# Order of the attention tiles in a hybrid decoder trunk: NSA, DSA, NSA, DSA in place of NSA, NSA, DSA, DSA

## The chip, the cores and the metric

The kernel runs on one core of a Trainium2 chip. The metric is the time of one execution on the device in microseconds, the median of three runs.

## The reference

Two layers work on 256 tokens of width 1024 in float32. A layer normalizes x (RMSNorm), projects it to 5472 columns, runs two causal token mixers side by side, adds their gated sum to x, and then adds a SwiGLU feed-forward of width 2816. The mixers, cut to what matters here:

```python
def _nsa_mixer(...):            # 8 heads, 2 key/value groups
    # compressed keys: 15 blocks of 32 tokens, stride 16; then the selected blocks and the window
    p_c = _masked_softmax(s_c, cmp_end <= t);  o_c = p_c @ vc
    p_s = _masked_softmax(q @ k_slc * ATTN_SCALE, causal);  o_s = p_s @ v_slc
    p_w = _masked_softmax(q @ k_win * ATTN_SCALE, causal);  o_w = p_w @ v_win
    return g0 * o_c + g1 * o_s + g2 * o_w

def _dsa_mixer(...):            # 8 heads
    # the indexer scores all keys, the best 64 of a query stay
    score = sum_h relu(iq_h @ ik) * iw_h;  sel = top_k(score, 64)
    return softmax(q @ k[sel] * ATTN_SCALE) @ v[sel]

def _hybrid_mixer(...):
    y_nsa = _nsa_mixer(...) @ w_branch_nsa
    y_dsa = _dsa_mixer(...) @ w_branch_dsa
    merged = sigmoid(gate_nsa) * y_nsa + sigmoid(gate_dsa) * y_dsa
    return merged @ w_out
```

With 256 tokens all four selection blocks are taken, and the window covers everything, so "selected" and "window" are plain causal attention over two sets of keys and values.

## The kernel before

The 256 tokens are two tiles of 128. Every large matrix product is made of three float32 matmuls: weights and activations are split into a high and a low half, and `mul3` (lines 194 to 196) issues high times high, low times high and high times low. ScalarE makes the high half of a weight tile (line 185), VectorE the low half (line 186). Raw weight tiles have five buffers, the halves four.

A layer's first part runs in this order of the source: the indexer's projection and the selection of keys, the projections of the NSA mixer, its compressed keys and values, the projections `dq`, `dk` and `dv` of the DSA mixer, then the attention itself, the projections of the two gates (line 727 evacuates them), the branch products (`branch`, `br` 0 for NSA and 1 for DSA; lines 749 and 751 evacuate them), and the output product.

`nsa(i)` handles one tile of tokens of the NSA mixer: the compressed scores (line 615), then groups of scores (line 368) into two PSUM banks `sc`, each followed by `softmax`; at the end the value matmuls (line 664 and, for the compressed part, line 667) into the only bank `yv`, and `y_out`, which splits the result into `ya` (lines 606, 607). The first tile sees 128 keys and makes four softmaxes, the second 256 keys and makes eight. `dsa(i)` does the same for the DSA mixer: scores (line 686 for the first tile, line 368 for the second), two softmaxes for the first tile and four for the second, value matmuls (line 703), `y_out`.

`softmax` is, on VectorE, a pass that adds the bias, scales and finds the maximum (line 330), on ScalarE the exponential with its sum (line 333), on VectorE the reciprocal and the scaling (lines 340, 342), then four transposes on TensorE (line 313) and their copy into a tile `pt` (line 314). There are eight tiles `pt`; a mixer's tile of tokens keeps its own until its value matmuls are done. The value matmuls of `nsa` begin with the `pt` that is made last.

The second tile of `dsa` multiplies split operands: `stack` and `twice` build `dks` and `dqs` (lines 351 to 362) in the memory of the tiles `qs` and `ks`, which `nsa` reads, so they can be written only when the last scores of `nsa(1)` are done. The first tile of `dsa` reads `dqT` and `dkT` unsplit and needs neither.

The order on each engine is made by a planner when the program is built: it takes what its own estimate says is ready, earlier lines of the source first. Blocks marked `manual_schedule` keep their order on TensorE among themselves; other work may come between.

Of the kernel before, what the change touches and what calls it, by code (L numbers as in the profile page):

```python
# [18 lines left out]
NT = SEQ // P  # L19
# [58 lines left out]
def hybrid_trunk(ctx: ExitStack, tc: tile.TileContext, a: dict, out: bass.AP):  # L78
# [17 lines left out]
    def yv_bank():  # L96
        return bank("yv", 1)
# [4 lines left out]
    def sc_bank():  # L102
        return bank("sc", 2)
# [216 lines left out]
    def softmax(segs, bias, gate):  # L320


        n, nb = len(segs), len(segs) and 4 // len(segs)
        pr = work.tile([P, n, nb * P], F32, tag="pr", name="pr", bufs=8)
        mx = small.tile([P, n], F32, tag="mx", name="mx")
        sm = small.tile([P, n], F32, tag="sm", name="sm")
        c = small.tile([P, n], F32, tag="c", name="c")
        b3 = bias.rearrange("p (b t) -> p b t", t=P)
        for h, v in enumerate(segs):
            nc.vector.tensor_tensor_reduce(pr[:, h].rearrange("p (b t) -> p b t", t=P), v, b3,  # L330
                                           -0.125, 3.4e38, ALU.add, ALU.min, accum_out=mx[:, h:h + 1])
        for h in range(n):
            nc.scalar.activation(pr[:, h], pr[:, h], AF.Exp, bias=mx[:, h:h + 1], scale=-1.0,  # L333
                                 accum_out=sm[:, h:h + 1])
        if gate is None:
            nc.vector.tensor_scalar_max(sm, sm, 1e-30)
        else:
            nc.vector.scalar_tensor_tensor(sm.rearrange("p (a b) -> p a b", b=2), sm.rearrange("p (a b) -> p a b", b=2),
                                           1e-30, gate, ALU.max, ALU.mult)
        nc.vector.reciprocal(c, sm)  # L340
        for h in range(n):
            nc.vector.tensor_scalar_mul(pr[:, h], pr[:, h], c[:, h:h + 1])  # L342
        pt = work.tile([P, 4, P], F32, tag="pt", name="pt", bufs=PTB)
        transpose_into(pt, [pr[:, h, b * P:(b + 1) * P] for h in range(n) for b in range(nb)])
        return pt
# [9 lines left out]
    def twice(dh, dl, src):  # L355

        for e in range(2):
            nc.scalar.activation(dh[e][HALF[e]], src[HALF[e]], AF.Copy)
            nc.any.tensor_copy(dh[e][HALF[1 - e]], src[HALF[e]])
        for e in range(2):  # L360
            for h in (e, 1 - e):
                nc.vector.tensor_sub(dl[e][HALF[h]], src[HALF[e]], dh[e][HALF[e]].bitcast(F32))

    def score(o, q, k):

        pairs = [(q, t) for t in k] if isinstance(k, (list, tuple)) else [(t, k) for t in q]
        for n, (u, v) in enumerate(pairs):
            nc.tensor.matmul(o, u, v, start=n == 0, stop=n == 1)  # L368
# [14 lines left out]
    for l in range(DEPTH):  # L383
# [220 lines left out]
        def y_out(bank, k0, tok):  # L604
            y3 = bank.rearrange("p (k t) -> p k t", t=P)
            nc.any.tensor_copy(ya[0][:, k0:k0 + 4, tok], y3)
            nc.vector.tensor_sub(ya[1][:, k0:k0 + 4, tok], y3, ya[0][:, k0:k0 + 4, tok].bitcast(F32))
# [60 lines left out]
                                 pct[:, 0], start=False, stop=r == 3)  # L668
            y_out(yn, 0, tok)

        def dsa(i):
            tok = slice(i * P, (i + 1) * P)
            nk = P * (i + 1)
            per = 512 // nk
            yd = yv_bank()

            done = []
            for p0 in range(0, 4, per):
                pts = []
                sbs = [sc_bank() for _ in range(2)]  # L680
                if i == 0:

                    with tc.manual_schedule(engines={nc.tensor.engine}):
                        for p in range(4):
                            for e in (1, 0):
                                nc.tensor.matmul(sbs[e][:, p * P:(p + 1) * P], dqT[HALF[e], p, 0:P],
                                                 dkT[HALF[e], p, 0:P], start=True, stop=True)
                else:
                    for p in range(p0, p0 + per):
                        for e in range(2):  # L690
                            score(sbs[e][:, (p - p0) * nk:(p - p0 + 1) * nk], [dqs[:, z, p] for z in (e, 2 + e)],
                                  dks[:, e, p])
                for sb in sbs:
                    segs = sb.rearrange("p (h b t) -> p h b t", h=per, t=P)
                    pts.append(softmax([segs[:, h] for h in range(per)], dbias[i], None))
                done.append((p0, pts))
            with tc.manual_schedule(engines={nc.tensor.engine}):
                for p in range(3, -1, -1):
                    p0, pts = done[p // per]
                    for b in range(i + 1):  # L700
                        for e in (1, 0):
                            v0 = (2 * p + e) * 64
                            nc.tensor.matmul(yd[e * 64:(e + 1) * 64, p * P:(p + 1) * P], dv[:, b, v0:v0 + 64],  # L703
                                             pts[e][:, (p - p0) * (i + 1) + b], start=p == 3 and b == 0,
                                             stop=p == 0 and b == i)
            y_out(yd, 4, tok)

        for i in range(NT):
            nsa(i)

        dks = one.tile([P, 2, 4, SEQ], F32R, tag="qs", name="dks")
        dqs = one.tile([P, 4, NT, 2 * P], F32R, tag="ks", name="dqs").rearrange("p z b (c t) -> p z (b c) t", t=P)
        stack([dks[:, e] for e in range(2)], dkT)
        twice([dqs[:, e] for e in range(2)], [dqs[:, 2 + e] for e in range(2)], dqT[:, :, P:])
        dsa(0)
        dsa(1)


        rhalf = []
# [186 lines left out]
```

## Time and profile before

| | |
|---|---|
| median of 3 runs | 800.53 us (799.58 to 800.77) |
| the profiled execution | 799.6 us, its span 797.8 us |
| TensorE, VectorE, ScalarE busy | 99%, 69%, 58% |
| mean granted clock of TensorE | 0.997 |

The span runs from the first to the last instruction of the profiled execution. PE is TensorE, PEld its weight loads, DVE VectorE, ACT ScalarE. Busy times of matmuls overlap, and their ends are modelled. In a timeline a row gives the start, how long the row lasts, the engine, the line, the operation, what it writes from what it reads, and how many instructions it joins. A row of windows gives the stretch, its length, then the busy time of PE, PEld, DVE, ACT and POOL with the number of instructions, the granted clock, the share of the DMA engines and GB/s; engines that a filtered answer doesn't have are left out.

### The profile page before, as it was taken

To read this page: it belongs to the slowest core of one execution; us is meant where nothing else is said; L and a number is where in the kernel's file an instruction comes from. 1 tells how busy PE (TensorE), PEld (TensorE's weight loads), DVE (VectorE), ACT (ScalarE), POOL (GpSimd) and SP (SyncE) were. 2 spreads that over 40 slices of the span, in tenths; PEclk is the share of its full clock that TensorE was granted. 3 is DMA by queue.
4 is the path that set the end of the run, shared out by engine and by line. 5 is a ranking of instruction groups with operands and counts; after the bars stand their busy time and mean duration, and the time that the engine had idled before them with its cause. 6 is when DMAs were issued, how large, how long until landed. Compare 5 with 4: busy or idle time off the path is not lost.

```text
span 797.8 us, 11520 instructions
## 1 busy us (share of the span) xinstructions
PE 788.3 (99%) x4122; PEld 655.3 (82%) x4122; DVE 547.0 (69%) x1187; ACT 460.5 (58%) x792; POOL 9.1 (1%) x18
## 2 busy tenths in 40 slices
PE   9999999999999999999999999999999999999996
PEld 6888888888888888888888888888888888888884
DVE  6789888967756455654567997989676555655544
ACT  6767577865645444543566756777557444545442
POOL 0100000000000000000000000000000000000000
PEclk9999999999999999999999999999999999999998
DMA  9964565324565556565468456442363666555651
GB/s 297 355 228 144 163 181 132 106 85 145 186 205 179 180 183 187 182 206 190 141 207 282 155 159 185 132 132 81 106 228 118 194 200 209 184 167 180 209 160 53
DMA packets 76282, 139.97 MB, mean 175 GB/s; under 512 B 7057, under 2 KB 22417, under 8 KB 76225
## 3 DMA queue, kind: packets, MB, share of 16 engines
q1 hardware_dynamic: 75120, 136.95, 55.0%
q10 hardware_dynamic: 864, 1.57, 0.5%
q0 software_dynamic: 240, 0.72, 0.3%
q8 instruction: 32, 0.52, 0.3%
q14 instruction: 26, 0.20, 0.1%
HBM read 138.17 MB, written 1.05 MB: 175 GB/s over the span
## 4 chain that ended last, share of the span: by engine, by line
PE 98%; DMA 0%; ACT 0%; DVE 0%; POOLq 0%; issue 0%; SPq 0%; ACTq 0%
PE mm L196 26%; PE mm L194 26%; PE mm L195 26%; PE tr L313 2%; PE sc L368 2%; PE yv L196 2%; PE yv L194 2%; PE yv L195 2%; PE yv L664 1%; PE tr L833 1%; PE yv L703 1%; PE tr L267 1%; PE yv L667 1%; PE sc L194 1%; PE sc L195 0%; PE sc L556 0%
## 5 line engine op out<-in xcount | busy, mean ns | idle before, releaser
L186 DVE TENSOR_TENSOR lo<-raw,hi 128x1024 fp32r<-128x1024 f32 (+2 forms) x252 | 299.5, 1195 | 140.8 <-ACT hi L185 135.6
L185 ACT ACTIVATE hi<-raw 128x1024 fp32r<-128x1024 f32 (+2 forms) x252 | 259.8, 1037 | 166.7 <-PE mm L196 112.6
L195 PE MATMUL mm<-lo,ah 128*128 128x512 f32 (+1 forms) x786 | 306.3, 390 | 0.0
L194 PE MATMUL mm<-hi,ah 128*128 128x512 f32 (+1 forms) x786 | 305.4, 394 | 0.0
L196 PE MATMUL mm<-hi,al 128*128 128x512 f32 (+1 forms) x786 | 305.3, 391 | 0.0
L196 PEld LDWEIGHTS mm<-hi,al 128*128 128x128 f32 x786 | 147.5, 188 | 29.6 <-issue 0.5
L195 PEld LDWEIGHTS mm<-lo,ah 128*128 128x128 f32 x786 | 147.8, 188 | 28.3 <-issue 0.3
L194 PEld LDWEIGHTS mm<-hi,ah 128*128 128x128 f32 x786 | 147.7, 188 | 28.3 <-issue 0.2
L333 ACT ACTIVATE pr<-pr,mx 128x128 f32<-128x128 f32 (+1 forms) x96 | 42.5, 445 | 11.4 <-DVE mx L330 11.1
L196 PE MATMUL mm<-hi,hl 128*128 128x512 f32 x126 | 49.1, 389 | 0.0
L195 PE MATMUL mm<-lo,hh 128*128 128x512 f32 x126 | 49.0, 389 | 0.0
L194 PE MATMUL mm<-hi,hh 128*128 128x512 f32 x126 | 48.8, 393 | 0.0
L838 DVE TENSOR_TENSOR hl<-tr,hh 128x512 fp32r<-128x512 f32 (+1 forms) x24 | 15.5, 647 | 38.3 <-ACT hh L837 38.3
L837 ACT ACTIVATE hh<-tr 128x512 fp32r<-128x512 f32 (+1 forms) x24 | 13.5, 562 | 47.2 <-PE tr L833 47.2
L196 PEld LDWEIGHTS mm<-hi,hl 128*128 128x128 f32 x126 | 23.6, 188 | 5.0
L195 PEld LDWEIGHTS mm<-lo,hh 128*128 128x128 f32 x126 | 23.7, 188 | 4.7
L194 PEld LDWEIGHTS mm<-hi,hh 128*128 128x128 f32 x126 | 23.7, 188 | 4.7
L342 DVE TENSOR_SCALAR pr<-pr,c 128x128 f32<-128x128 f32 (+1 forms) x96 | 25.1, 315 | 0.6
L824 ACT ACTIVATE sg<-mm,rstd 128x512 f32<-128x512 f32 (+1 forms) x24 | 15.7, 654 | 10.5 <-PE mm L196 8.7
L330 DVE CUSTOM_DVE_ANT_0 pr<-sc,cst 128x128 f32<-128x128 f32 (+1 forms) x64 | 19.5, 352 | 2.6 <-PE sc L368 2.4
L314 ACT COPY pt<-tr 128x512 f32<-128x512 f32 x32 | 17.7, 584 | 4.9 <-PE tr L313 4.7
L313 PE MATMUL tr<-cst,pr 128*128 128x128 f32 x144 | 20.0, 272 | 0.0
(237 smaller groups left out, 757.8 us busy)
## 6 DMA issues: line engine op xcount, KB each, us to landing
raw<-w_in SPq DMA_DIRECT2D x76, 512.0 KB, 4.0
raw<-w_ffn_down SPq DMA_DIRECT2D x44, 512.0 KB, 4.1
raw<-w_ffn_gate SPq DMA_DIRECT2D x40, 512.0 KB, 4.5
raw<-w_ffn_up SPq DMA_DIRECT2D x40, 512.0 KB, 4.3
raw<-w_out SPq DMA_DIRECT2D x16, 512.0 KB, 4.5
raw<-w_branch_nsa SPq DMA_DIRECT2D x16, 256.0 KB, 4.0
raw<-w_branch_dsa SPq DMA_DIRECT2D x8, 512.0 KB, 3.6
raw<-w_in SPq DMA_DIRECT2D x8, 280.0 KB, 3.9
```

Source lines behind the costliest of these rows:

```text
L185: nc.scalar.activation(hi[:, cs], raw[:, cs], AF.Copy)
L186: nc.vector.tensor_sub(lo[:, cs], raw[:, cs], hi[:, cs].bitcast(F32))
L194: nc.tensor.matmul(dst, xh, wh, start=first, stop=False)
L195: nc.tensor.matmul(dst, xh, wl, start=False, stop=False)
L196: nc.tensor.matmul(dst, xl, wh, start=False, stop=last)
L313: nc.tensor.transpose(tp[:, k * P:(k + 1) * P], piece, ident)
L314: nc.any.tensor_copy(dst, tp[:, 0:len(parts) * P].rearrange("p (k t) -> p k t", t=P))
L330: nc.vector.tensor_tensor_reduce(pr[:, h].rearrange("p (b t) -> p b t", t=P), v, b3, -0.125, 3.4e38, ALU.add, ALU.min, accum_out=mx[:, h:h ...
L333: nc.scalar.activation(pr[:, h], pr[:, h], AF.Exp, bias=mx[:, h:h + 1], scale=-1.0, accum_out=sm[:, h:h + 1])
L342: nc.vector.tensor_scalar_mul(pr[:, h], pr[:, h], c[:, h:h + 1])
L368: nc.tensor.matmul(o, u, v, start=n == 0, stop=n == 1)
L824: nc.scalar.activation(s[:, 0:n], dg[i][:, 0:n], AF.Silu, scale=rstd[i])
```

## The change

The four attention tiles are called in the order NSA first token tile, DSA first, NSA second, DSA second. Before, both tiles of NSA came first. The stacked copies `dks` and `dqs` are still made after the second tile of NSA, and `dsa` gets them as arguments, since its first call now stands ahead of them. Both layers are changed alike.

```diff
-        def dsa(i):
+        def dsa(i, dqs=None, dks=None):
...
-        for i in range(NT):
-            nsa(i)
+        nsa(0)
+        dsa(0)
+        nsa(1)
 
         dks = one.tile([P, 2, 4, SEQ], F32R, tag="qs", name="dks")
         dqs = one.tile([P, 4, NT, 2 * P], F32R, tag="ks", name="dqs").rearrange("p z b (c t) -> p z (b c) t", t=P)
         stack([dks[:, e] for e in range(2)], dkT)
         twice([dqs[:, e] for e in range(2)], [dqs[:, 2 + e] for e in range(2)], dqT[:, :, P:])
-        dsa(0)
-        dsa(1)
+        dsa(1, dqs, dks)
```

## Rows read from the trace of the kernel before

**Rows 1.** The page: busy engines and the clock in 40 slices.
```profile
PE 788.3 (99%) x4122; PEld 655.3 (82%) x4122; DVE 547.0 (69%) x1187; ACT 460.5 (58%) x792; POOL 9.1 (1%) x18
...
PEclk9999999999999999999999999999999999999998
```

**Rows 2.** Timeline of TensorE: the opening, and the projections near 98 us.
```profile
1.19 3.64 PE L110 MATMUL tr<-zeros 128*128 128x512 bf16 x10 [1.19 <-DVE warm L135]
...
98.17 0.39 PE L195 MATMUL mm<-lo,ah 128*128 128x512 f32 x1
98.40 0.39 PE L196 MATMUL mm<-hi,al 128*128 128x512 f32 x1
```

**Rows 3.** All waits of TensorE: us in total, times, longest.
```profile
PE tr L110 <- DVE warm L135: 1.2, 1, 1.2
PE sc L194 <- ACT hi L185: 0.7, 1, 0.7
```

**Rows 4.** Windows: the opening, and two stretches of layer 1's attention.
```profile
0.00:3.90 3.90, 2.71 (x7) 1.04 (x8) 0.43 (x7) 1.27 (x1) 0.20 (x4) 1.00 0.49 162
...
93.00:143.00 50.00, 50.00 (x284) 41.93 (x282) 40.18 (x148) 36.38 (x94) 0.00 (x0) 1.00 0.54 148
143.00:160.00 17.00, 17.00 (x99) 14.28 (x100) 16.75 (x57) 14.67 (x39) 0.00 (x0) 1.00 0.38 125
```

**Rows 5.** Windows of the tiles "mm" alone (PE, PEld, DVE, ACT).
```profile
151.90:160.50 8.60, 6.24 (x25) 4.06 (x23) 0.00 (x0) 0.69 (x1) 1.00 0.56 183
```

**Rows 6.** Timeline of TensorE around the attention pieces, layers 1 and 2.
```profile
142.90 0.48 PE L686 MATMUL sc<-gb,ga 64*128 64x128 f32 x2
143.31 0.50 PE L194 MATMUL mm<-hi,ah 128*128 128x512 f32 x1
...
148.07 1.16 PE L686 MATMUL sc<-gb,ga 64*128 64x128 f32 x14
149.15 0.50 PE L195 MATMUL mm<-lo,ah 128*128 128x512 f32 x1
...
153.38 0.60 PE L313 MATMUL tr<-cst,pr 128*128 128x128 f32 x4
153.73 0.48 PE L195 MATMUL mm<-lo,ah 128*128 128x512 f32 x1
...
159.51 1.20 PE L368 MATMUL sc<-dks,dqs 128*128 128x256 f32 x8
160.63 3.71 PE L664 MATMUL yv<-pt,ga 128*64 128x128 f32 x64
...
165.27 1.04 PE L313 MATMUL tr<-cst,pr 128*128 128x128 f32 x8
166.11 0.50 PE L194 MATMUL mm<-hi,ah 128*128 128x512 f32 x1
...
167.67 1.09 PE L703 MATMUL yv<-pt,ga 128*64 128x128 f32 x16
...
553.17 3.71 PE L664 MATMUL yv<-pt,ga 128*64 128x128 f32 x64
```

**Rows 7.** Timeline of ScalarE: the last "pt" of NSA second, both layers.
```profile
158.62 0.56 ACT L314 COPY pt<-tr 128x512 f32<-128x512 f32 x1
...
550.93 0.56 ACT L314 COPY pt<-tr 128x512 f32<-128x512 f32 x1
```

**Rows 8.** Groups of VectorE, 93 to 180 us: busy us, mean ns, idle before.
```profile
L342 DVE TENSOR_SCALAR pr<-pr,c 128x128 f32<-128x128 f32 x24 | 5.3, 281 | 0.1
...
L607 DVE TENSOR_TENSOR al<-yv,ah 128x512 fp32r<-128x512 f32 x4 | 2.8, 691 | 5.5 <-ACT ah L606 5.5
...
L330 DVE CUSTOM_DVE_ANT_0 pr<-sc,ga 128x128 f32<-128x128 f32 x8 | 1.8, 283 | 0.0
```

**Rows 9.** Timeline of VectorE: the stacked copies.
```profile
143.81 0.85 DVE L359 CAST dqs<-ga 64x512 fp32r<-64x512 f32 x2
144.68 2.45 DVE L353 TENSOR_TENSOR dks<-gb,dks 64x1024 fp32r<-64x1024 f32 x2
147.15 2.79 DVE L362 TENSOR_TENSOR dqs<-ga,dqs 64x512 fp32r<-64x512 f32 x4
```

## The prediction

> **What bounds the kernel now.** I read the page first. TensorE is busy 99% of the span, VectorE 69%, and the clock was granted at nearly full level in every slice [rows 1]. A busy TensorE says little by itself, because its records overlap: a 512-column matmul is shown as 0.39 us long, while the next one starts 0.23 us later [rows 2]. So I went to the starts, and to the waits of TensorE. The whole trace holds two waits, both in the first six microseconds, 1.9 us together [rows 3]. In both attention stages TensorE never waits. The reader should keep that in mind for everything below: the time is the sum of what TensorE issues, and an order can save none of it, except where small matmuls pack better; it can only add a wait.
>
> Then the windows. From 93 to 143 us TensorE is busy 50.00 of 50.00, VectorE 40.18, ScalarE 36.38; from 143 to 160, where NSA second ends, DSA first runs and DSA second begins, VectorE is busy 16.75 of 17.00 [rows 4]. So TensorE bounds the stage, and VectorE is the engine that could take its place.
>
> Why TensorE never waits there is seen in what it does between the attention pieces: 512-column matmuls of the gate projections and, at the end, of the first NSA branch. They are the cover. It is thin at one place. From 151.9 to 160.5 us only 25 matmuls of the group "mm" are left [rows 5]: 24 of them are NSA branch, first token tile, 24 x 0.23 = 5.5 us. The NSA branch of the second tile needs the output of NSA second, and the four weight pairs that it holds keep the DSA branch's weights out (the pools hi and lo have four buffers). So when the probability-times-value matmuls of NSA second start at 160.63 [rows 6], TensorE has nothing else to do. Its last transposed probabilities landed at 158.62 + 0.56 = 159.18 [rows 7]: 1.45 us to spare. In layer 2 they land at 550.93 + 0.56 = 551.49 [rows 7], and the matmuls start at 553.17 [rows 6]: 1.68 us.
>
> **The change, part by part.**
> Removed and added: nothing. Both loops issue the same instructions, the same DMAs and the same tiles, and the two stacked copies dks and dqs are built behind NSA second as before. TensorE's sum changes by 0.
>
> Moved on TensorE: DSA first, that is 16 score matmuls, 8 transposes and 16 value matmuls. Today its scores stand in two pieces, 2 at 142.90 (0.41 us until the next start) and 14 at 148.07 (1.08 us) [rows 6]. In one piece, at 1.08/14 = 0.077 each, the two would cost 0.15, so 0.26 less in a layer. Eight transposes in one group hold 0.84 us (165.27 to 166.11), four 0.35 us (153.38 to 153.73) [rows 6], so a group of eight that is split saves 0.14 and two that are merged lose it; there are five groups of eight in layer 1's stage. The bound for the packing is thus -0.26 - 5 x 0.14 = -0.96 us a layer, and the same the other way. I take 0: which pieces merge depends on a planner that sees other things.
>
> Moved on VectorE: eight first passes over the scores, 1.8 us, eight scalings at 5.3/24 = 0.22, 1.8 us, and the low half of the output, 0.69: 4.3 us in a layer [rows 8]. It goes from the full stretch (16.75 of 17.00) into one with 9.8 us idle [rows 4]. Of those some 4.3 are wanted. If every idle moment serves, the cost is 0; if none does, NSA second and the weight splits behind it are 4.3 us later. The nearest row is the idle total, more than twice the need, so I take nearly 0, and keep 4.3 for the range.
>
> Queues that are passed: on VectorE and ScalarE everything of NSA second now stands behind DSA first. SP's queue is not passed: DSA first has no DMA. The eight buffers of the transposed probabilities are shared, so DSA first holds two until its value matmuls are done; NSA second needs all eight. Before, the two of DSA first had to wait for NSA second's value matmuls (their eight transposes come at 165.27, behind 160.63) [rows 6]; this wait goes. It hid under the NSA branch's second tile and so frees no time of TensorE.
>
> The new edge: the stacked copies now have no DSA first between them and their reader. They take VectorE from 143.81 to 149.94 [rows 9]. The second DSA tile then starts its scores without cover of its own, but TensorE has the value matmuls of NSA second (160.63 to 165.27, 4.6 us), 5.5 us of the NSA branch's second tile, and, new, 5.5 us of the DSA branch's first tile, since DSA first is done. That covers it; I take 0.
>
> Sum: the profiled execution took 799.6 us, span 797.8. Work 0, packing 0, and 0.3 us for both layers together as small waits at the thin place: 799.9. The median of the runs lies 0.9 above the profiled execution, so 800.8.
>
> **The rivals.**
> A, the thin place opens. If DSA first pushes the last probabilities of NSA second by its whole 4.3 us, they land at 159.18 + 4.3 = 163.5. TensorE gets there at 160.63 plus DSA first's transposes and value matmuls, which now come earlier (0.84 + 1.09 [rows 6]), so at 162.6: a wait of 0.9. If the scores of DSA second (two groups of eight, up to 1.20 each [rows 6]) fall behind as well, it gets there at 160.2 and waits 3.3. For two layers 1.8 to 6.6: 802.3 to 807.1, middle 804.7. For it: the margin of 1.45 us is less than 4.3. Against it: from 143.81 VectorE works 6.1 us on the copies and then on DSA first before it comes back to NSA second [rows 9], so the end of NSA second is late by order, not by need, and the second half of that is what moves away. It decides from a delay of 1.45 + 1.93 = 3.4 us on.
>
> B, VectorE becomes the bound earlier. If DSA first fills none of its idle time from 93 to 143, the low halves of the weights come 4.3 us late and TensorE waits for them: up to 8.6 us in all, 809.1. For it: 80% busy already. Against: 4.3 into 9.8, and ScalarE is busy 36.38 of 50 only [rows 4].
>
> C, faster: the packing bound, -0.96 in each layer, 798.6 on the scale of the median. Nothing else can give time, for there is no wait to take away [rows 3]. For it: the split scores. Against: it needs all groups to fall well.
>
> D, nothing happens: the planner orders by readiness, and the source's order is only a preference, so DSA first might stay about where it was. Then 800.5.
>
> E, the clock. The granted clock is 1.00, the level of 2.4 GHz, in every window of [rows 4], and no wait stands in the trace that could have lowered it. The Trainium skill (TensorE: Matmul & The Clock Gate, HAM oscillation) says that a long idle of TensorE in mid-kernel brings the lower level back; no row here shows that. The slowest row of like matmuls is the opening, where ten of 512 columns hold 3.64 us, 0.36 each against 0.23 later [rows 2]. If a long wait were followed by 4 us at that pace, it would cost 4 x (1 - 0.23/0.36) = 1.4 more, in both layers 2.9, on top of B: 812.0.
>
> **Numbers.** Forecast 0.50, A 0.22, B 0.12, C 0.07, D 0.07, E 0.02. The likeliest gives 800.8. Less than 0.2% (1.6 us) can't be told from no change here: the three runs lie 0.15% apart. Same: forecast and D, 0.57. Slower: A, B and E, 0.36. Faster: C, 0.07. The range runs from just above C to the upper end of A, 798.9 to 807.1; B's end and E lie outside. The likeliest alone spans 799.5 to 802.0.
>
> **What would show it.** Right: no wait of TensorE in either attention stage; DSA first's value matmuls before NSA second's; VectorE fuller than 80% from 93 to 143 and less full behind. Wrong by A: a wait of TensorE's value matmuls of NSA second for a copy of the probabilities. Wrong by B: waits of weight loads for the low halves. Wrong by C: a span shorter by over a microsecond with the same matmul count. A difference that lies outside the two attention stages would be none of these.

## The result and the profile after

The changed order takes 805.78 us (median of 6 runs, 804.62 to 807.91) against 799.47 us for the kernel before (6 runs on the same chip, 799.29 to 800.77): the ratio is 1.0079, with a 95% interval of 1.0069 to 1.0088. It is slower by 6.3 us. That lies inside the predicted range, but the case held likeliest, no change, is wrong, and the sum behind the range is not the one that was measured. The profiled execution took 807.42 us with a span of 805.7, which is 7.9 us more than the span of before, 797.8.

The page of the kernel after, its head, its busy engines and the clock in slices:

```profile
span 805.7 us, 11523 instructions
...
PE 792.8 (98%) x4122; PEld 658.1 (82%) x4122; DVE 548.0 (68%) x1186; ACT 461.0 (57%) x793; POOL 9.2 (1%) x18
...
PEclk9999999989999999999999999999999999999999
```

The matmul count is that of [rows 1], so nothing was added. One slice of the clock shows an 8, and it is the ninth, which runs from 161 to 181 us: the end of layer 1's attention. The share of busy TensorE hardly moves, which again tells little; the list of waits tells more. All waits of TensorE in the kernel after (us in total, times, longest), against the two of [rows 3]:

```profile
PE sc L368 <- DVE dqs L362: 1.8, 2, 1.0
PE yv L664 <- ACT pt L314: 1.4, 2, 0.8
PE tr L110 <- DVE warm L135: 1.2, 1, 1.2
PE mm L195 <- DVE lo L186: 0.7, 1, 0.7
PE sc L194 <- ACT hi L185: 0.6, 1, 0.6
PE sc L368 <- DVE c L340: 0.4, 1, 0.4
```

The lines for "warm" and "hi" are the opening again. The other four are new, and all stand in attention: 1.8 + 1.4 + 0.7 + 0.4 = 4.3 us. Next, TensorE from the first of them on, kernel after:

```profile
153.85 0.71 PE L368 MATMUL sc<-ks,qs 128*128 128x512 f32 x2
...
159.90 0.39 PE L196 MATMUL mm<-hi,al 128*128 128x512 f32 x1
160.12 0.40 PE L368 MATMUL sc<-dks,dqs 128*128 128x256 f32 x2
161.49 0.62 PE L368 MATMUL sc<-dks,dqs 128*128 128x256 f32 x3 [0.97 <-DVE dqs L362]
162.91 0.62 PE L368 MATMUL sc<-dks,dqs 128*128 128x256 f32 x3 [0.80 <-DVE dqs L362]
163.88 1.95 PE L368 MATMUL sc<-dks,dqs 128*128 128x256 f32 x8 [0.35 <-DVE c L340]
165.63 1.05 PE L313 MATMUL tr<-cst,pr 128*128 128x128 f32 x4
167.36 5.67 PE L664 MATMUL yv<-pt,ga 128*64 128x128 f32 x64 [0.68 <-ACT pt L314]
172.96 1.16 PE L667 MATMUL yv<-pct,gb 128*128 128x128 f32 x8
```

The reader is to see the order. All sixteen scores of DSA second (160.12 to 165.6) stand in front of the value matmuls of NSA second (167.36), and TensorE issues in that order. So it first waits for the copies that the scores read (0.97 and 0.80), then 0.35 for VectorE, then for NSA second's last probabilities (0.68). VectorE in the same stretch, kernel after:

```profile
154.60 0.42 DVE L330 CUSTOM_DVE_ANT_0 pr<-sc,cst 128x256 f32<-128x256 f32 x1 [0.16 <-PE sc L368]
...
155.41 0.85 DVE L359 CAST dqs<-ga 64x512 fp32r<-64x512 f32 x2
156.30 1.22 DVE L186 TENSOR_TENSOR lo<-raw,hi 128x1024 fp32r<-128x1024 f32 x1
157.55 2.47 DVE L353 TENSOR_TENSOR dks<-gb,dks 64x1024 fp32r<-64x1024 f32 x2
160.05 2.80 DVE L362 TENSOR_TENSOR dqs<-ga,dqs 64x512 fp32r<-64x512 f32 x4
162.89 0.16 DVE L338 SCALAR_TENSOR_TENSOR sm<-sm,eg 128x2 f32<-128x2 f32 x1
```

One block of work is late for both. The copies, 155.41 to 162.85, hold back the scores that read them. They also stand in front of the last softmax of NSA second: VectorE reads its scores at 154.60 and comes back to its sums only at 162.89. That order is not new. VectorE in the kernel before, the sums of the same softmax, right behind the copies of [rows 9]:

```profile
149.97 0.16 DVE L338 SCALAR_TENSOR_TENSOR sm<-sm,eg 128x2 f32<-128x2 f32 x1
```

What is new is that the whole group comes 12.9 us later, while TensorE runs out of other work at about the same time: it reaches the scores of DSA second at 160.12, and before it reached the value matmuls of NSA second at 160.63 [rows 6].

Why does NSA second end so close to the copies? Before, its last scores were issued at 142.25; now at 153.85, 11.6 us later. The delay is there from its first instruction on. TensorE in the kernel before, the start of NSA second (L615) and its last scores:

```profile
113.49 0.97 PE L615 MATMUL sc<-kcbd,ga 128*128 128x32 f32 x8
...
142.25 0.71 PE L368 MATMUL sc<-ks,qs 128*128 128x512 f32 x2
```

TensorE in the kernel after, the scores of DSA first (L686) and the start of NSA second:

```profile
113.42 0.49 PE L686 MATMUL sc<-gb,ga 64*128 64x128 f32 x2
...
119.64 0.93 PE L686 MATMUL sc<-gb,ga 64*128 64x128 f32 x10
...
121.09 0.49 PE L686 MATMUL sc<-gb,ga 64*128 64x128 f32 x4
...
126.65 0.97 PE L615 MATMUL sc<-kcbd,ga 128*128 128x32 f32 x8
```

VectorE in the kernel after, the last reading of those scores:

```profile
123.11 0.29 DVE L330 CUSTOM_DVE_ANT_0 pr<-sc,ga 128x128 f32<-128x128 f32 x1
```

DSA first takes both score banks at once and writes them alternately. It holds them from 113.42, when the first comes free, until VectorE has read its scores, at 123.40. NSA second starts only behind that, at 126.65 instead of 113.49. The wait for the banks is not all of these 13.2 us: NSA first's last reading of a bank ends at 114.83, the scores of DSA first go on only at 119.64, and 3.2 us lie between 123.40 and 126.65. In both gaps TensorE works on other matmuls in the order that the planner chose, and no run tells why it chose so. It is not VectorE's lack of time. Windows of the kernel after (us, then busy us of PE, PEld, DVE, ACT and POOL, the granted clock, DMA share and GB/s), to be held against [rows 4]:

```profile
93.00:143.00 50.00, 50.00 (x299) 41.28 (x298) 38.70 (x145) 34.57 (x93) 0.00 (x0) 1.00 0.52 144
143.00:160.00 17.00, 17.00 (x88) 14.05 (x87) 15.72 (x47) 14.40 (x33) 0.00 (x0) 1.00 0.42 123
...
164.60:171.40 6.80, 6.09 (x46) 5.72 (x48) 5.98 (x28) 3.63 (x13) 0.00 (x0) 0.50 0.00 1
```

VectorE is busy 38.70 us from 93 to 143, less than the 40.18 of before. The last row is the other part of the loss: right behind the waits the clock was granted at 0.50, the level of 1.2 GHz, for 6.8 us. If the 6.8 us less the 0.68 us of waiting in them were work at half pace, they cost some 3.1 us (an estimate from these rows). 4.3 + 3.1 = 7.4 of the 7.9 us. By the first addition of the output product to x on VectorE (L803: 203.01 before, 210.06 after; in layer 2 595.54 and 604.26), 7.05 us are lost in layer 1 and 1.7 in layer 2, where a wait of 0.7 for a low half and one of 0.8 for the probabilities stand and the clock holds; 0.8 us is made up behind. In layer 1 the four waits (2.8 us) and the clock (3.1) leave 1.2 us that no row places.

### The profile page after: what moved, and what is told of

Its sections match the earlier page's. It is cut to its first block, busy times and chain, and to the rows that moved or that the text cites. A ratio compares the mean times of both kernels' runs of the same rounds, so it can differ in the third digit from the quotient of the medians.

```text
span 805.7 us, 11523 instructions
## 1 busy us (share of the span) xinstructions
PE 792.8 (98%) x4122; PEld 658.1 (82%) x4122; DVE 548.0 (68%) x1186; ACT 461.0 (57%) x793; POOL 9.2 (1%) x18
## 4 chain that ended last, share of the span: by engine, by line
PE 96%; DVE 2%; ACT 1%; DMA 0%; issue 0%; POOLq 0%; SPq 0%; DVEq 0%; ACTq 0%
PE mm L194 26%; PE mm L196 26%; PE mm L195 26%; PE tr L313 2%; PE sc L368 2%; PE yv L194 2%; PE yv L196 2%; PE yv L195 2%; PE yv L664 2%; PE tr L833 1%; PE yv L703 1%; DVE dqs L362 1%; PE tr L267 1%; PE yv L667 1%; PE sc L194 0%; PE sc L195 0%
## 5 line engine op out<-in xcount | busy, mean ns | idle before, releaser
L837 ACT ACTIVATE hh<-tr 128x512 fp32r<-128x512 f32 (+1 forms) x24 | 13.5, 562 | 47.2 <-PE tr L833 47.2
L313 PEld LDWEIGHTS tr<-cst,pr 128*128 128x128 f32 x144 | 17.4, 143 | 3.1 <-issue 0.3
```

What stands on the lines that cost most here:

```text
L313: nc.tensor.transpose(tp[:, k * P:(k + 1) * P], piece, ident)
```

## Experiments

All were timed beside the kernel before on the same chip; its medians there were 799.55 to 799.67 us. Unless said otherwise, the short diffs are against the kernel after.

**The change once more (after_again).** No edit.

> The changed kernel unaltered, for a second profile. If the lowered clock of layer 1 (0.50 from 164.6 to 171.4 us) is a consequence of the waits that comes and goes with the execution, this profile has it elsewhere, longer, shorter or not at all, and the span moves by the 2 to 3 us that it costs. If it belongs to the order as such, it stands at the same place with the same length.

805.92 us, ratio 1.0080 (1.0061 to 1.0099); span 804.1. The waits are the same, but the clock was low for half as long. Window of this execution:

```profile
163.90:167.30 3.40, 2.90 (x12) 2.53 (x12) 3.29 (x19) 2.74 (x11) 0.00 (x0) 0.50 0.00 0
```

3.4 us in place of 6.8, and the span is 1.6 us shorter: half of the difference, as half pace would have it. So the waits are the steady part of the loss, and the clock a part that varies between executions. The ten executions on record bear this out: those of 804.58 to 804.76 us have a mean granted clock of 0.998 to 0.999, those of 807.42 to 807.91 one of 0.994. Not all of the spread is the clock, for one of 805.87 has 0.999 too. Even the fastest is 5.1 us above the 799.47 of the kernel before.

**Without the copies (e_nocopy).** DSA second's scores read tensors that lie ready, so the stacked copies are left out.

```diff
-        dks = one.tile([P, 2, 4, SEQ], F32R, tag="qs", name="dks")
-        dqs = one.tile([P, 4, NT, 2 * P], F32R, tag="ks", ...
-        stack(...)
-        twice(...)
+        dks = qs
+        dqs = ks.rearrange("p z b (c t) -> p z (b c) t", t=P)
```

> The changed kernel without the copies dks and dqs: DSA second reads the operands of the NSA mixer in their place, which have the same shapes, so 6.1 us of VectorE and 3.4 us of ScalarE go in each layer and the output is not the reference's. Theory 'copies in front' (the copies stand ahead of NSA second's last softmax and of DSA second's scores): the waits of TensorE in the attention stages go, 3.5 to 4.6 us of them in the profile to under 1, and the time falls to 799 to 801. Theory 'banks' (DSA first holds the two score banks for 12 us, so NSA second ends 11.6 us later and that alone empties the cover): waits of over 2 us stay, 803 to 806. Theory 'VectorE load' (the 4.3 us of DSA first): between, 801 to 803.

798.92 us, ratio 0.9991 (0.9982 to 1.0001). That is the case of 'copies in front', just below its 799 to 801. TensorE waits only in the opening. NSA second is as late as in the kernel after; its last scores and the start of its value matmuls here:

```profile
154.03 0.71 PE L368 MATMUL sc<-ks,qs 128*128 128x512 f32 x2
...
163.19 0.98 PE L664 MATMUL yv<-pt,ga 128*64 128x128 f32 x14
```

The late end of NSA second alone costs nothing. It costs when the copies are there too.

**Half of the copies (e_half).** Only dks, 2.47 us of VectorE and its share of ScalarE, is left out; dqs is made.

```diff
-        dks = one.tile(...)
-        stack(...)
+        dks = qs
```

> The changed kernel with the copies dqs made and the copies dks left out (DSA second reads the NSA queries in their place, so the output is not the reference's): 2.45 us of VectorE and 2.1 us of ScalarE less in each layer. Theory 'both': the waits of layer 1 (2.8 us in front of DSA second's scores and NSA second's value matmuls) fall by about these 2.1 to 2.5 us, to under 1 us, no fall of the clock, 799.5 to 802. If the copies mattered by their order alone and not by their length, the waits stay over 2 us, 803 to 807.

799.98 us, ratio 1.0005 (0.9996 to 1.0015); the only wait behind the opening is one of 0.2. The sums of NSA second's last softmax on VectorE in this run:

```profile
159.71 0.16 DVE L338 SCALAR_TENSOR_TENSOR sm<-sm,eg 128x2 f32<-128x2 f32 x1
```

They stand 3.2 us earlier than in the kernel after (162.89), and the value matmuls follow at 163.05 without a wait. A third of the block of 7.4 us taken away (with 2.1 us of ScalarE) is enough: in this layer the kernel after is past its edge by at most some 3 us, not by the whole block.

**Other banks for DSA first (e_mm).** Its scores go to the banks of the projections, and the score banks stay with NSA.

```diff
-                sbs = [sc_bank() for _ in range(2)]
+                sbs = [(mm_bank if i == 0 else sc_bank)() for _ in range(2)]
```

> The changed kernel with the scores of DSA first in two banks of the pool mm in place of the two banks sc. Theory 'banks': NSA second's first scores come up to 12 us earlier, its last near 143 as before the change, the waits go, 799 to 801. Theory 'copies in front': the copies still stand ahead of the last softmax, so waits of over 2 us stay, 803 to 806. Theory 'VectorE load': VectorE does the same work, NSA second ends 4.3 us later than before the change, 801 to 804. If both the delay and the copies are needed for the wait, this and the kernel without copies are both back at 799 to 801.

802.02 us, ratio 1.0029 (1.0017 to 1.0041). TensorE's scores of DSA first, the start of NSA second, its last scores and its value matmuls:

```profile
90.56 1.16 PE L686 MATMUL mm<-gb,ga 64*128 64x128 f32 x16
...
107.08 0.97 PE L615 MATMUL sc<-kcbd,ga 128*128 128x32 f32 x8
...
132.81 1.17 PE L368 MATMUL sc<-ks,qs 128*128 128x512 f32 x4
...
162.55 3.71 PE L664 MATMUL yv<-pt,ga 128*64 128x128 f32 x64
```

And the waits of TensorE in this run:

```profile
PE sc L368 <- DVE mx L330: 1.3, 2, 0.6
PE tr L110 <- DVE warm L135: 1.2, 1, 1.2
PE sc L576 <- DVE hid L573: 1.0, 1, 1.0
PE mm L686 <- ACT ga L317: 0.6, 1, 0.6
```

The time alone missed the 799 to 801 of 'banks' and lies in the 801 to 804 of 'VectorE load'; the trace decides. That theory has NSA second 4.3 us later than before. Here it starts at 107.08, its last scores come 21 us earlier than in the kernel after and 9.4 us earlier than in the kernel before, its value matmuls 4.8 us earlier than after, and the waits in front of them are gone. So the shared score banks go with the delay, and VectorE's work does not. The edit moves more than the banks, though: the planner now puts DSA first at 90.56, ahead of NSA first. How many of the 13.2 us each bank costs is thus not shown. The kernel is still 0.3% slower than before, because the edit brings 2.9 us of waits of its own, and one of them (0.6 for `ga`) is for the inputs of DSA first, which now starts while they are being made.

**The scores of DSA first without a fixed order (e_free).** They may be written bank by bank.

```diff
-                    with tc.manual_schedule(engines={nc.tensor.engine}):
+                    if True:
```

> The changed kernel without the fixed order of DSA first's score matmuls; the planner then issues them bank by bank (four of one bank, later four of the other) in place of one, five and two, so the first bank can be read before the second is free. Theory 'both' (NSA second's delay by the two banks and the copies in front of it are needed together, as the kernels without copies and with other banks showed): if NSA second starts at least 4 us earlier than the 126.7 us of the changed kernel, the waits shrink below 1 us in each layer and the time is 800 to 802; if it starts where it did, waits and time stay, 804 to 808. Theory 'copies alone': 804 to 808 in either case.

811.40 us, ratio 1.0145 (1.0131 to 1.0159): outside what was expected. NSA second starts at 127.2, no earlier. The first bank got its scores from 113.95 on, but VectorE read neither bank before 121.80, so the alternating order was not what held the banks. The waits for the copies doubled, since they now stand in both layers (3.5 us in 4 waits for dqs, 0.7 for c, 0.7 for pt, 0.5 for pr), and the clock was low for 3.4 us in layer 1 and 6.8 in layer 2. Why layer 2 waits for the copies in this kernel and not in the kernel after stays open.

**DSA first ahead of everything (e_d0).**

```diff
-        nsa(0)
         dsa(0)
+        nsa(0)
         nsa(1)
```

> The order DSA first, NSA first, NSA second, DSA second, copies as they were. DSA first has its operands near 92 us, when VectorE is idle (4.9 us busy of 8 from 93 to 101), and the banks are then not yet wanted by NSA. Theory 'both': NSA second starts nearer to 113 than to 127, the tail has no wait, 799.5 to 803, the rest being waits where DSA first delays the compressed keys, as with the banks of the pool mm. Theory 'copies alone': waits of over 2 us at NSA second's value matmuls, 803 to 807.

800.08 us, ratio 1.0006 (0.9997 to 1.0015). NSA second starts at 120.60, its last scores come at 149.28, between the 142.25 of before and the 153.85 of after. The time is that of 'both', two of its signs are not: the start is no nearer to 113 than to 127, and the tail of layer 1 keeps one wait for the probabilities, as long as in the kernel after (0.68). The waits for `dqs` are gone. The waits behind the opening:

```profile
PE yv L664 <- ACT pt L314: 0.7, 1, 0.7
PE mm L195 <- DVE lo L186: 0.6, 1, 0.6
PE tr L313 <- ACT pr L333: 0.3, 1, 0.3
```

**No copies, the scores formed another way (e_plain, and e_plain_before on the kernel before).** DSA second's scores are formed like those of DSA first, from dqT and dkT at once, and need no copies. The diff is shortened: the scores also get the fixed order that those of DSA first have, and the lines that make the copies go.

```diff
-                            score(sbs[e][:, ...], [dqs[:, z, p] for z in (e, 2 + e)], dks[:, e, p])
+                            nc.tensor.matmul(sbs[e][:, ...], dqT[HALF[e], p, P:2 * P],
+                                             dkT[HALF[e], p], start=True, stop=True)
```

> The changed kernel with DSA second's scores computed as those of DSA first are, from dqT and dkT unsplit, so that the copies dks and dqs are not made at all. Theory 'both': no wait of TensorE in the attention stages, as without the copies, and a time of 798.5 to 800.5. TensorE's own cost: 16 split matmuls of 256 columns held 1.9 to 2.4 us; 16 unsplit ones of 128 columns held 1.1 to 1.5, so with 256 columns 2.2 to 3; at most 1 us more in each layer. Theory 'VectorE load': waits remain, 801 to 803.

> The kernel before with the same edit, the copies dks and dqs not made. No wait is there to be taken away, so by every theory the time changes by TensorE's own cost alone: 798.5 to 801. If it comes out below the changed kernel with this edit, the order costs something beside the waits; if both are equal within 0.2%, the order itself costs nothing once the copies are gone.

801.90 us (1.0028, 1.0018 to 1.0038) in the new order and 801.82 us (1.0027, 1.0016 to 1.0038) in the old. Both lie above what was expected (up to 800.5 and 801), since the unsplit scores cost 2.2 us and not at most 2. The order on top of them costs 0.1 us, which is nothing that can be told apart. The last scores of NSA second in the new order without copies:

```profile
153.98 0.71 PE L368 MATMUL sc<-ks,qs 128*128 128x512 f32 x2
```

They are as late as in the kernel after, and TensorE waits nowhere behind the opening. The order harms only through the copies.

**The copies behind the last probabilities (e_late).** Two corners of the copies are first written from the two probability tiles that NSA second makes last in the program, so that the copies must come after these.

```diff
-        nsa(1)
+        last = nsa(1)
+        nc.vector.tensor_copy(dks[:, :, 0, 0:1], last[0][:, 0:2, 0:1])
+        nc.vector.tensor_copy(dqs[:, :, 0, 0:1], last[1][:, 0:4, 0:1])
```

> The changed kernel with the copies dks and dqs put behind the last two pt of NSA second (two small VectorE copies of a corner make them wait). Theory 'copies in front': NSA second's value matmuls no longer wait for pt, they start near 160 in layer 1; the copies now run under them and under the NSA branch's second tile; time 800 to 803. Theory 'banks' or 'VectorE load': the value matmuls of NSA second are late as before and the copies come later still, so 806 to 812.

807.46 us, ratio 1.0099 (1.0083 to 1.0115): no gain, 0.2% above the kernel after. That is the time which 'banks' and 'VectorE load' were given, but the run does not decide for them, since the edit did only part of what it was for. Two rows of VectorE in this run, the first corner and the sums of the last softmax:

```profile
155.41 0.16 DVE L715 CAST dks<-pt 128x2 fp32r<-128x2 f32 x1
...
157.69 0.16 DVE L338 SCALAR_TENSOR_TENSOR sm<-sm,eg 128x2 f32<-128x2 f32 x1
```

And two of TensorE, the value matmuls of NSA second and transposes of DSA second:

```profile
162.38 3.71 PE L664 MATMUL yv<-pt,ga 128*64 128x128 f32 x64 [0.68 <-ACT pt L314]
...
181.19 0.63 PE L313 MATMUL tr<-cst,pr 128*128 128x128 f32 x4 [1.80 <-DVE pr L342]
```

The planner had made those two tiles early, by 155.4, so the copies moved by 0.3 to 1.4 us. But the last softmax now slipped in between them (157.69 in place of 162.89), and the value matmuls of NSA second went ahead of most of DSA second's scores, at 162.38 in place of 167.36. What was gained there was lost behind: DSA second came late in its turn, and TensorE waited 1.80 us for its probabilities at 181.19, then 0.49, 0.24 and 0.69 up to 186.38. The wait was not removed, only passed on. New waits of 5.4 us explain most of the 7.1 us of span above before; the rest I can't place.

**The old order with the copies made twice (e_twice_before, against the kernel before).**

```diff
+        for _ in range(2):
             stack(...)
             twice(...)
```

> The kernel before, its order NSA, NSA, DSA, DSA untouched, with the copies dks and dqs made twice over (the same values again, 6.1 us of VectorE and 3.4 us of ScalarE more in each layer). Theory 'both': the old order is safe only by its early NSA second; 6.1 us more ahead of its last softmax exceeds the 1.45 us that it has to spare, so TensorE waits 2 to 5 us in a layer for the first time, 803 to 812. Theory 'order': the waits come from the new order alone, and the old one has DSA first to cover the copies; under 1 us of waits, 799 to 801.

805.41 us, ratio 1.0078 (1.0061 to 1.0095). Waits:

```profile
PE sc L368 <- DVE dqs L362: 2.6, 4, 0.8
PE mm L194 <- ACT gb L728: 1.6, 2, 0.9
```

The time is that of 'both', the place of the waits is not: TensorE was to wait at NSA second's value matmuls, and these start at 161.67 without a wait. VectorE did the sums of NSA second's last softmax between the two sets of copies, so the second set does not stand ahead of it as a block and the 1.45 us were not put to the test:

```profile
150.50 0.16 DVE L338 SCALAR_TENSOR_TENSOR sm<-sm,eg 128x2 f32<-128x2 f32 x1
```

What waits are the scores of DSA second for the second `dqs`, as in the kernel after, and matmuls of the gates for ScalarE (`gb`), which makes part of the copies too. So the kernel before is within one set of copies of an edge itself. Whether DSA first, which stood between the copies and their reader, was its cover is not shown.

## Why the prediction was right in its range and wrong in its steps

**What bounds the kernel, and that an order can only add a wait: right.** No new order came out below before by more than its interval; e_nocopy, at 0.9991, does so little even though it leaves work out.

**The cover is thin at NSA second's value matmuls: right.** That is the place where rival A puts the wait, and the wait for the copy of the probabilities stands there in both layers. That its size there (0.68 and 0.8) is near A's smaller figure, 0.9, is luck: A has the probabilities land at 163.5 and TensorE arrive at 162.6, and both came some 4 us later. ScalarE in the kernel after, the last `pt` of NSA second:

```profile
166.72 0.58 ACT L314 COPY pt<-tr 128x512 f32<-128x512 f32 x1 [0.66 <-PE tr L313]
```

**"Moved on VectorE … I take nearly 0, and keep 4.3 for the range": the first failed step.** It is right that VectorE has the time. It even was less full from 93 to 143 (38.70 of 50, where over 80% was named as a sign), because NSA second moved out. But the delay of NSA second was never VectorE's to set. Its last scores come 11.6 us later, and with them goes the planner's order around two score banks which the prediction lists nowhere among the "queues that are passed"; it names the probability buffers only. Shown by e_mm, where DSA first is moved even further ahead and takes the same passes on VectorE, but from other banks, and NSA second's scores come early. One argument against A held: DSA first no longer stands in NSA second's last stretch. From its last scores to its last probabilities it takes 13.5 us (153.85 to 167.30) in place of 16.9 (142.25 to 159.18), so the probabilities are 8.1 us late, not 11.6. A's own condition, a delay of more than 3.4 us, was still met twice over.

**"The new edge … That covers it; I take 0": the second failed step, and the one that made the loss.** The value matmuls of NSA second and the branches behind them were named as cover for DSA second's scores. TensorE issued those scores ahead of the cover (160.12 against 167.36), so it could not serve. The copies were also taken at their old time, 143.81 to 149.94; they need NSA second's last scores, and ended at 162.85. That they stand ahead of NSA second's last softmax is said under A, but not that they would be late with it. e_nocopy and e_plain (no wait with NSA second just as late) and e_mm and e_d0 (no wait for the copies with the copies in place and NSA second earlier) show that both conditions are needed.

**Rival B, VectorE as the bound: refuted.** e_nocopy gives VectorE the same DSA first as early and loses nothing. One wait for a weight's low half did come, B's own sign, but of 0.7 us in layer 2 only.

**Rival E, the clock: occurred, though without the long wait it asks for.** The prediction put the price at 1.4 us a layer; the two executions give at most 1.7 (half of 3.4 us) and about 3.1. Its pace was taken from the opening, whose window shows the full level [rows 4]; at the low level work ran at half pace, and up to 6.8 us of it. It came in layer 1 alone.

**Packing, C, and D: not seen.** DSA first moved where the source put it. Its scores came in three pieces instead of two; without copies the two orders are 0.1 us apart (e_plain and e_plain_before), so packing is worth nothing that can be told apart.

So A had the right sign and one of the right places, and 805.78 lies in its interval of 802.3 to 807.1, which sets the upper end of the range. That it does so is partly luck, since the measured sum has terms that A lacks: 1.8 for the copies, 1.4 for the probabilities, 1.1 for the rest, and up to 3.1 for the clock.

## What to carry to other kernels

When a block of work is moved past another, list the buffers that both take, accumulation banks above all: the later one can be late by far more than the work that engines do for the earlier (here 13.2 us at its start, against 4.3 us of VectorE's work). Cover counts only if the engine issues it ahead of the instruction that waits (here 4.6 us of value matmuls stood behind it, and covered nothing); look up what stands ahead in program order, and follow a late block to every reader and to everything queued behind it. And a kernel without waits can still be at an edge: double the suspect (here the copies in the old order) to see how far off it is.

## What was not expected of the hardware

The granted clock fell to 0.50 at 164.60 us for 6.8 us, behind three waits of 0.97, 0.80 and 0.35 us that lie within some 4 us, none of them as long as the opening's 1.19; in the second execution of the same kernel it fell at the same place for 3.4 us. In the profiled executions it did not fall behind the waits of 1.80, 0.49, 0.24 and 0.69 us of e_late, which end within some 5 us, nor in e_twice_before with four waits for `dqs` of at most 0.8 and two of at most 0.9 for `gb`. The Trainium skill (TensorE: Matmul & The Clock Gate, A second HAM failure mode: psum-queue depth-cycling) says that frequent short idles between groups of matmuls can make the clock swing between its two levels; the falls here agree in kind, though the idles come from a late copy, and the two kernels without a fall show that short idles alone are not enough. What tells the runs with a fall from those without was not settled.

Small matmuls at the low level show the price directly: the 64 value matmuls of NSA second were busy for 5.67 us in the profile after, where 4.0 us of them lay at 0.50, and for 3.71 us in [rows 6].
